# The last block's residual is added by TensorE in PSUM, and the reload's copies move behind the root

## The chip, the cores and the metric

The kernel runs on one core of a Trainium2 chip. The metric is the device time of one execution in microseconds (us), the median of several runs. In the profile PE is TensorE (PEld its weight loads), DVE is VectorE, ACT is ScalarE, POOL is GpSimd and SP is SyncE, which here issues most of the DMAs. The DMA engines are 16. "Granted clock" is the share of full clock that PE got.

## What is computed

One inference step of a two-layer streaming encoder, in float32, over 1024 prompt positions and 64 sample positions (1088 columns) of 1024 channels. Layer 0 mixes tokens by sliding-window attention, layer 1 by a diagonal state-space model; each layer then has a gated ConvFFN. Around each of the four parts stand two norms, one before, and one after it whose result is added to the residual:

```python
def rms_norm(x, g):
    x32 = x.astype(jnp.float32)
    y = x32 * lax.rsqrt(jnp.mean(x32 * x32, axis=-1, keepdims=True) + NORM_EPS) * g.astype(jnp.float32)
    return y.astype(x.dtype)
...
        hp = rms_norm(xp, g_pre_mix[i])
        ...
            mp, hrp, hip = s5_mixer(hp, h0, h0, *ssm_params)
        xp = xp + rms_norm(mp, g_post_mix[i])
        hp = rms_norm(xp, g_pre_ffn[i])
        fp, cpi = conv_ffn(hp, jnp.zeros((bp, CONV_WIDTH - 1, 2 * D_FF), hp.dtype), w_up[i], conv_w[i], conv_b[i], w_down[i])
        xp = xp + rms_norm(fp, g_post_ffn[i])
```

The change concerns two of these places: the end of layer 0 (the last line, then the first norm of layer 1, whose result the state-space mixer reads), and the end of layer 1, whose last line gives the output.

## The kernel before

Channels lie on the 128 partitions, as eight tiles `k` of 128 channels; the columns are cut into three blocks `b` of 384, 384 and 320. All weight products are float32, made of three products of a split in two parts (`mm3`, lines 224 to 226). The program is built once in Python; a scheduler then sets the order on each engine from its own estimate of times, from priorities and from `self.order(x, first)`, which puts x behind first without a wait of its own. Each engine runs its instructions in that order.

`down` ends the FFN of block 2: its last products go to PSUM tiles tagged `mm` (six buffers), and DVE adds them to `y` (L658). Then `post_norm` runs. It loads the residual in four pairs of tiles, `xs`. `rstd` squares y pair by pair on ACT (L255, L249), sums the pairs on DVE (L257, L247, L250), lets PE sum over the partitions by products with `ones` (L267, into `pr`), takes the root (L271 on ACT, where `root` is true) and refines the reciprocal on DVE (L272 to L292), and spreads it over the partitions with three transposes (L285). ACT scales y by the gain (L321). `apply` multiplies y by `pr` (L329, one pair an instruction) and adds `xs` (L332): in block 2 ahead of the mixer all four adds are DVE's, at the end the second and fourth are DVE's and the first and third POOL's; at the end each pair is then stored (L336).

Ahead of the mixer (`pre == 4` in `f`), `ssm_bounce` copies the sum into `xs[q]`, the pair's tiles with the columns in another order (L1140 on ACT for block 2), and writes them to memory `hd` (L1146); `ssm_load(q)` reloads them as `U` (L1195), 16 channels by 8 steps on the partitions. All of this is for raw values; `ssm_norm` runs a second `rstd` over the sum, spreads the root with small products (L1182, `pr<-sel`) into `rs` (L1184, L1185), and DVE multiplies `U` by it (L1203). `fill` issues products with the identity whose result nobody reads (`idle`): eight of 512 columns behind the transposes, one behind the statistics, one of 256 columns behind the small products.

The mixer then goes through 32 pairs of groups, mostly two pairs a batch: PE forms the inputs (L1258, p1), DVE scans (L1289 to L1310), PE forms the outputs (L1318, L1324), ACT copies them to `ys` (L1332). `pm` are their parameters (L1222). For each eighth of the channels `ys` is written to memory `yd` and reloaded as `yf`; ACT applies the GELU (`z`, L1359) and splits it, `zh` on ACT (L1368) and `zl` on DVE (L1372). The products of the GLU follow, then the second FFN, whose end is the end of the program.

Of the kernel before, what the change touches and what calls it, by code (L numbers as in the profile page):

```python
# [43 lines left out]
class Core:  # L44
# [193 lines left out]
    def rstd(self, src, n, tag, root, bcast=True, first=False, alt=None, adder=None, fine=False):  # L238
# [3 lines left out]
        for q in range(4):  # L242
            sq = self.n2(n, tag)
# [8 lines left out]
            if first:  # L252
                nc.gpsimd.tensor_mul(sq, xq, xq)
            else:
                self.sq[q] = nc.scalar.activation(sq, xq, AF.Square)  # L255
            if q:
                adder.tensor_add(acc, acc, sq)  # L257
            else:
                acc = sq
        else:  # L260
            adder.tensor_add(acc[:, 0], acc[:, 0], acc[:, 1])
# [8 lines left out]
        if root:  # L270
            nc.scalar.activation(x, st, AF.Sqrt, bias=self.eps)  # L271
# [40 lines left out]
    def post_norm(self, y, b, g, xsrc, root, roomy, out=None, by=None):  # L312
# [12 lines left out]
        def apply():  # L325
            last = None
            for q in range(4):
# [792 lines left out]
    def ssm_bounce(self, xt, b, qs=range(4), after=None):  # L1120
# [9 lines left out]
        for q in qs:  # L1130
            for u, v, c in segs:
                o = self.xs[q][:, :, :, c:c + (v - u) // 8]
                (pk, nk), (ps, ns), (pc, n_) = o.ap[1:]
                o = bass.AP(tensor=o.tensor, offset=self.xs[q][:, 0, 7, c:c + 1].offset, ap=[o.ap[0], [pk, nk], [pc, n_], [-ps, ns]])
                x = xt[:, 2 * q:2 * q + 2, u:v].rearrange("p k (c s) -> p k c s", s=8)
                if b < 2:
                    r = self.rn[:, 384 * b:384 * b + 384].rearrange("p (c s) -> p c s", s=8)
                    nc.vector.tensor_mul(o, x, r[:, None].to_broadcast([P, 2, 48, 8]))
                    continue
                x = nc.scalar.activation(o, x, AF.Copy)  # L1140
                if after is not None:
                    self.order(x, after[(0, 1, 3, 3)[q]])
            if b == 2:
                for k in ([0], [1]) if q == 0 else ([0, 1],):
                    r = self.hd[(2 * q + k[0]) * P:(2 * q + k[-1] + 1) * P].rearrange("(k p) s c -> p k (s c)", p=P)
                    self.hw[q] = nc.sync.dma_start(r, self.xs[q][:, k[0]:k[-1] + 1].rearrange("p k s c -> p k (s c)"))  # L1146
# [7 lines left out]
    def ssm_norm(self, xt, b):  # L1154
# [23 lines left out]
        self.fill(idle, 1, 512, self.last_st)  # L1178
        for i, c in enumerate(range(0, n, P)):
            c = min(c, n - P) // 8  # L1180
            nc.vector.tensor_scalar(ex[:, 16 * i:16 * i + 16], self.dsel, r[:, i:i + 1], None, op0=ALU.mult)
# [23 lines left out]
    def ssm(self, after):  # L1205
# [4 lines left out]
        with tc.tile_pool(name="ss", bufs=1) as sp:  # L1210
# [36 lines left out]
            def batch(qs):  # L1247
# [267 lines left out]
def build(tc, a):  # L1515
    nc = tc.nc
    with ExitStack() as ctx:
# [28 lines left out]
        def then(post, xs, xo, pre):  # L1546
# [62 lines left out]
```

## Time and profile before

| | |
|---|---|
| median of 3 runs | 2239.77 us (2237.23 to 2244.5) |
| the profiled execution, its own time | 2241.03 us |
| its span, first to last instruction | 2239.2 us |
| instructions in the span | 35982 |
| busy share PE, DVE, ACT, POOL | 98%, 74%, 47%, 18% |
| mean granted clock of PE | 0.992 |
| first FFN's last product | 1170.21 us |
| the mixer's first input products | 1190.3 us |
| last input products | 1279.9 us |
| last product of the second FFN | 2224.42 us |

Times in rows are us from the span's start. A row of a time line reads: start, length, engine, line, operation, out<-in, shape, count, and in brackets the idle time of that engine before it with what ended it. A row by stretches reads: stretch, its length, busy time of the engines asked for with the number of instructions, granted clock, DMA share, GB/s. A row of DMA issues ends with the size of one and the time to landing. On PE a float32 product counts as two instructions in the time line.

### The profile page before, as it was taken

What the parts mean: (1) busy time and instruction counts of PE and PEld (TensorE: products, weight loads), DVE (VectorE), ACT (ScalarE), POOL (GpSimd) and SP (SyncE); (2) the same over time, 40 slices, a digit from 0 to 9 for tenths busy, and PEclk for the clock granted to TensorE, in tenths of its full rate; (3) what the DMA queues carried; (4) which work ended last, traced back from release to release, by engine and by line L of the source; (5) the groups of instructions that cost most, each with busy time, mean ns of one, the idle gap of its engine ahead of it and who ended that gap; (6) DMA issues with size and microseconds to landing.
All of it is one profiled execution on the core that took longest, in us unless ns stands there. A gap on an engine that the chain in (4) does not pass through costs nothing.

```text
span 2239.2 us, 35982 instructions
## 1 busy us (share of the span) xinstructions
PE 2191.6 (98%) x13875; PEld 2117.1 (95%) x13875; DVE 1661.3 (74%) x2886; ACT 1042.3 (47%) x1890; POOL 412.8 (18%) x474
## 2 busy tenths in 40 slices
PE   9999999999999999999988899999999999999997
PEld 8987789999999999999986699999999999999997
DVE  8687647989878877767758855597976776676764
ACT  5255747422343342555545641263555455455543
POOL 5322004200032423000200034352010110110000
PEclk9999999999999999999999899999999999999999
DMA  5100015655355565887749888752266686579772
GB/s 197 37 22 29 20 62 158 241 188 202 122 150 173 176 208 187 274 279 236 233 163 339 263 280 294 249 167 75 87 224 229 218 297 226 196 272 314 218 253 97
DMA packets 208123, 428.47 MB, mean 191 GB/s; under 512 B 23312, under 2 KB 114224, under 8 KB 205008
## 3 DMA queue, kind: packets, MB, share of 16 engines
q1 hardware_dynamic: 175648, 326.56, 44.2%
q0 software_dynamic: 23984, 95.12, 11.9%
q10 hardware_dynamic: 8320, 4.49, 0.8%
q8 instruction: 109, 1.79, 0.3%
q14 instruction: 62, 0.51, 0.1%
HBM read 297.75 MB, written 128.37 MB: 190 GB/s over the span
## 4 chain that ended last, share of the span: by engine, by line
PE 32%; DMA 13%; DVE 9%; issue 4%; ACT 2%; POOL 2%; SPq 0%; DVEq 0%; ACTq 0%; POOLq 0%
PE mm L224 10%; PE mm L226 10%; PE mm L225 10%; DMA sj<-in_w_up 3%; DMA raw<-in_w_down 2%; DMA jw<-in_w_down 2%; DMA raw<-sd 1%; POOL sj L1391 1%; DMA yd<-ys 1%; DVE whl L217 1%; DMA su<-sj 1%; DMA gd<-t 1%; DVE gt L564 1%; DVE t L425 1%; DMA yf<-yd 1%
## 5 line engine op out<-in xcount | busy, mean ns | idle before, releaser
L224 PE MATMUL mm<-hl,whl 128*128 128x384 f32 (+1 forms) x1960 | 643.3, 329 | 4.1 <-DVE hl L307 3.1
L226 PE MATMUL mm<-hh,whl 128*128 128x384 f32 (+1 forms) x1960 | 641.2, 329 | 2.3 <-DVE whl L217 2.3
L225 PE MATMUL mm<-hh,whl 128*128 128x384 f32 (+1 forms) x1960 | 643.1, 328 | 0.0
L224 PEld LDWEIGHTS mm<-hl,whl 128*128 128x128 f32 x1960 | 368.4, 188 | 6.5 <-DVE hl L307 4.7
L226 PEld LDWEIGHTS mm<-hh,whl 128*128 128x128 f32 x1960 | 368.4, 188 | 3.0 <-DVE whl L217 2.9
L225 PEld LDWEIGHTS mm<-hh,whl 128*128 128x128 f32 x1960 | 368.6, 188 | 0.1
L217 DVE TENSOR_TENSOR whl<-raw,whl 128x1024 fp32r<-128x1024 f32 x202 | 254.9, 1263 | 146.7 <-ACT whl L217 146.2
L217 ACT ACTIVATE whl<-raw 128x1024 fp32r<-128x1024 f32 x202 | 213.0, 1058 | 248.1 <-PE mm L226 128.6
L224 PE MATMUL mm<-gt,whl 128*128 128x384 f32 (+1 forms) x968 | 316.8, 327 | 2.9 <-ACT whl L217 2.4
L226 PE MATMUL mm<-gt,whl 128*128 128x384 f32 (+1 forms) x968 | 315.8, 327 | 0.7 <-DVE whl L217 0.7
L225 PE MATMUL mm<-gt,whl 128*128 128x384 f32 (+1 forms) x968 | 315.9, 327 | 0.0
L224 PEld LDWEIGHTS mm<-gt,whl 128*128 128x128 f32 x968 | 181.7, 188 | 3.7 <-ACT whl L217 2.6
L226 PEld LDWEIGHTS mm<-gt,whl 128*128 128x128 f32 x968 | 181.7, 188 | 1.2 <-DVE whl L217 1.2
L225 PEld LDWEIGHTS mm<-gt,whl 128*128 128x128 f32 x968 | 181.8, 188 | 0.0
L195 DVE TENSOR_TENSOR whl<-raw,whl 128x1024 fp32r<-128x1024 f32 x84 | 96.4, 1154 | 72.7 <-ACT whl L194 71.3
L424 DVE SCALAR_TENSOR_TENSOR t<-u,ppt,t 128x1090 f32<-128x1090 f32 x88 | 126.9, 1443 | 5.8 <-ACT t L423 4.1
L194 ACT ACTIVATE whl<-raw 128x1024 fp32r<-128x1024 f32 x84 | 82.6, 987 | 101.8 <-DMA raw<-sd 40.1
L423 ACT ACTIVATE t<-u,ppt 128x1090 f32<-128x1090 f32 x88 | 114.2, 1298 | 26.2 <-DVE u L520 13.6
L425 DVE SCALAR_TENSOR_TENSOR t<-u,ppt,t 128x1090 f32<-128x1090 f32 x88 | 122.0, 1386 | 0.4
L415 DVE TENSOR_TENSOR u<-rb,mm 128x384 f32<-128x384 f32 (+1 forms) x164 | 80.8, 504 | 31.2 <-PE mm L226 26.4
L438 ACT ACTIVATE t<-t 128x1090 f32<-128x1090 f32 x44 | 49.1, 1115 | 113.1 <-DVE t L425 113.1
L564 DVE TENSOR_TENSOR gt<-gr,gt 128x768 fp32r<-128x768 f32 (+2 forms) x106 | 90.5, 881 | 11.1 <-ACT gt L563 10.2
(389 smaller groups left out, 4141.5 us busy)
## 6 DMA issues: line engine op xcount, KB each, us to landing
raw<-in_w_up SPq DMA_DIRECT2D x88, 512.0 KB, 4.4
raw<-in_w_down SPq DMA_DIRECT2D x74, 512.0 KB, 4.4
raw<-sd SPq DMA_DIRECT2D x40, 512.0 KB, 4.9
sj<-in_w_up POOLq DMA_DIRECT2D x68, 256.0 KB, 6.1
su<-sj POOLq DMA_DIRECT2D x34, 512.0 KB, 5.9
raw<-su SPq DMA_DIRECT2D x34, 512.0 KB, 4.6
pm<-prm SPq DMA_DIRECT2D x32, 522.0 KB, 8.2
gr<-td SPq DMA_DIRECT2D x40, 384.0 KB, 5.6
```

Of the source, the lines that this page charges most:

```text
L194: nc.scalar.activation(w[:, 0], raw, AF.Copy)
L195: nc.vector.tensor_sub(w[:, 1], raw, w[:, 0].bitcast(F32))
L217: x = nc.scalar.activation(w[:, 0], raw, AF.Copy), nc.vector.tensor_sub(w[:, 1], raw, w[:, 0].bitcast(F32))
L224: nc.tensor.matmul(out, w[:, 0, sl], xl, start=start, stop=False, skip_group_check=more)
L225: nc.tensor.matmul(out, w[:, 0, sl], xh, start=False, stop=False, skip_group_check=more)
L226: self.last_mm = nc.tensor.matmul(out, w[:, 1, sl], xh, start=False, stop=stop, skip_group_check=more)
L415: nc.vector.tensor_mul(u[:, t0 + 2:t0 + 2 + np_], rb[:, t0:t0 + np_], ps[:, :np_])
L423: nc.scalar.activation(t, u[:, 0:T + 2], AF.Identity, bias=cb(m), scale=cw(0, m))
L424: nc.vector.scalar_tensor_tensor(t, u[:, 1:T + 3], cw(1, m), t, op0=ALU.mult, op1=ALU.add)
L425: self.last_conv = nc.vector.scalar_tensor_tensor(t, u[:, 2:T + 4], cw(2, m), t, op0=ALU.mult, op1=ALU.add)
L438: nc.scalar.activation(ta, ta, AF.Gelu_apprx_tanh)
L564: nc.vector.tensor_sub(x[:, 1, u], raw, x[:, 0, u].bitcast(F32))
```

## The change

In block 2 ahead of the mixer and at the end (`own`) PE adds the residual for most tiles. `post_norm` takes PSUM tiles `ad` (six, at the end five); a product of the residual with the identity starts each of them, and in `apply` a product of the multiplied y with the identity is added. At the end ACT copies these tiles back to y; the rest is added by DVE, and POOL adds nothing there any more. Ahead of the mixer the second `rstd` squares the six tiles straight from PSUM, and DVE's adds of the first three pairs, which still have to reach y, stand behind the sums (first pair) and behind the small products' operands (second and third). The first tile is copied for the reload from PSUM, all others behind the root. Idle products: six of 512 columns behind the last product of y in place of eight behind the transposes, two behind the statistics in place of one. The `rd` tiles of the first batches stand behind `rs`.

```diff
-    def rstd(self, src, n, tag, root, bcast=True, first=False, alt=None, adder=None, fine=False):
+    def rstd(self, src, n, tag, root, bcast=True, first=False, alt=None, adder=None, fine=False, ads=()):
...
-            sq = self.n2(n, tag)
+            sq = self.n2(n, "sqb" if ads and q % 2 else tag)
+            if ads and q < 3:
+
+                for j in range(2):
+                    ahead = nc.scalar.activation(sq[:, j], ads[2 * q + j], AF.Square)
+                if q:
+                    adder.tensor_add(acc, acc, sq)
+                else:
+                    acc = sq
+                continue
...
+            if ads:
+                self.order(self.sq[q], ahead)
...
+        own = roomy and b == 2
+        ads = [self.mm_ps("ad")[:, :n] for _ in range(6 if out is None else 5)] if own else []
+
+        def residual(ks, first):
+            for k in ks:
+                self.order(nc.tensor.matmul(ads[k], self.ident, xs[k // 2][:, k % 2], start=True, stop=False), first)
+        if own:
+            residual(range(3), self.last_mm)
         pr, _ = self.rstd(y, n, "sqa", root, alt=b % 2 if roomy else None, fine=b == 2)
+        if own:
+            residual((3, 4), self.last_st)
+            residual(range(5, len(ads)), self.last_tr)
...
+            if own:
+                for q in range(4):
+                    yq = y[:, 2 * q:2 * q + 2]
+                    V.tensor_mul(yq, yq, pr[:, None, :n].to_broadcast([P, 2, n]))
+                    for k in range(2 * q, min(2 * q + 2, len(ads))):
+                        self.last_ad = nc.tensor.matmul(ads[k], self.ident, y[:, k], start=False, stop=True)
+                        if out is not None:
+                            nc.scalar.activation(y[:, k], ads[k], AF.Copy)
+                    if q == 3:
+                        if len(ads) < 6:
+                            V.tensor_add(y[:, 5], y[:, 5], xs[2][:, 1])
+                        V.tensor_add(yq, yq, xs[q])
+                for q in range(4 if out is not None else 0):
+                    nc.sync.dma_start(out[:, 2 * q:2 * q + 2], y[:, 2 * q:2 * q + 2])
+                return ads, xs
...
-    def ssm_bounce(self, xt, b, qs=range(4), after=None):
+    def ssm_bounce(self, xt, b, qs=range(4), ahead=None):
...
+            k0, k1 = (0, 2) if q or b < 2 else (0, 1) if ahead is not None else (1, 2)
...
-                x = nc.scalar.activation(o, x, AF.Copy)
-                if after is not None:
-                    self.order(x, after[(0, 1, 3, 3)[q]])
+                x = ahead[:, None] if ahead is not None else xt[:, 2 * q + k0:2 * q + k1]
+                x = nc.scalar.activation(o, x[:, :, u:v].rearrange("p k (c s) -> p k c s", s=8), AF.Copy)
+                if ahead is None:
+                    self.order(x, self.last_root)
...
+        ads, xs = last if b == 2 else ((), ())
+        ps, r = self.rstd(xt, n, "sqa" if b == 2 else "sqb", True, bcast=b < 2, alt=1 - b % 2, adder=nc.gpsimd if b == 0 else None, ads=ads)
         if b == 2:
-            idle = self.mm_ps("idle")
-            self.fill(idle, 8, 512, self.last_tr)
-        ps, r = self.rstd(xt, n, "sqa" if b == 2 else "sqb", True, bcast=b < 2, alt=1 - b % 2, adder=nc.gpsimd if b == 0 else None)
+            idle = self.sm_ps("idle", 0)
+            self.fill(idle, 6, 512, self.last_ad)
+            xq = xt[:, 0:2]
+            self.order(nc.vector.tensor_add(xq, xq, xs[0]), self.last_add)
...
-        self.fill(idle, 1, 512, self.last_st)
+        self.fill(idle, 2, 512, self.last_st)
...
+        for q in (1, 2):
+            xq = xt[:, 2 * q:2 * q + 2]
+            self.order(nc.vector.tensor_add(xq, xq, xs[q]), e)
...
-                    if out[0]:
-                        self.order(x, out[0])
+                    self.order(x, out[0] or self.last_rs)
...
-                c.post_norm(y, b, g(post), xs[b], post != 5 or b == 2, post in (3, 7), xo[b] if pre is None else None,
-                            {3: "1111", 7: "0101"}.get(post) if b == 2 else None)()
+                last = c.post_norm(y, b, g(post), xs[b], post != 5 or b == 2, post in (3, 7), xo[b] if pre is None else None)()
                 if pre == 4:
                     if b == 2:
-                        c.ssm_bounce(y, b, [0])
-                    c.ssm_norm(y, b)
+                        c.ssm_bounce(y, b, [0], ahead=last[0][0])
+                    c.ssm_norm(y, b, last)
                     if b == 2:
-                        c.ssm_bounce(y, b, range(1, 4), dict(c.sq))
+                        c.ssm_bounce(y, b, range(4))
```

On PE between the FFN's last product and the mixer stood (`xl` is the residual's tile, `ad` its sum's PSUM tile):

```order
L226 MATMUL mm<-gt,whl 128x320
L267 MATMUL pr<-ones,sqa 128x1 x3
L285 MATMUL pr<-ident,nvsqa 128x128 x3
L231 MATMUL idle<-ppt,ident 128x512 x8
L267 MATMUL pr<-ones,sqa 128x1 x3
L231 MATMUL idle<-ppt,ident 128x512
L1182 MATMUL pr<-sel 128x16 x3
L231 MATMUL idle<-ppt,ident 128x256
```

and stands now:

```order
L226 MATMUL mm<-gt,whl 128x320
L335 MATMUL ad<-xl,ident 128x320 x3
L278 MATMUL pr<-ones,sqa 128x1 x3
L335 MATMUL ad<-xl,ident 128x320 x2
L296 MATMUL pr<-ident,nvsqa 128x128 x3
L335 MATMUL ad<-xl,ident 128x320
L354 MATMUL ad<-y,ident 128x320 x6
L231 MATMUL idle<-ppt,ident 128x512 x6
L278 MATMUL pr<-ones,sqa 128x1 x3
L231 MATMUL idle<-ppt,ident 128x512 x2
L1224 MATMUL pr<-sel 128x16 x3
L231 MATMUL idle<-ppt,ident 128x256
```

Twelve products of 320 columns are new, and the second statistics stand behind the six idle products, which follow the last product of y.

On SP, the writes and reloads of the four pairs (`xs_10757` to `xs_10760` are pairs 0 to 3) stood, for the two first reloaded tiles:

```order
L1146 DMA hd_10756<-xs_10757 128x1096 x2
L1195 DMA U_11558<-hd_10756 128x8x137
L1146 DMA hd_10756<-xs_10758 128x2x1096
L1195 DMA U_11558<-hd_10756 128x8x137
L1146 DMA hd_10756<-xs_10759 128x2x1096
L1146 DMA hd_10756<-xs_10760 128x2x1096
L1195 DMA U_11563<-hd_10756 128x8x137 x2
L1222 DMA pm_11566<-prm_292 128x1044 x2
```

and stand now:

```order
L1185 DMA hd_10756<-xs_10757 128x1096
L1240 DMA U_11580<-hd_10756 128x8x137
L1185 DMA hd_10756<-xs_10757 128x1096
L1185 DMA hd_10756<-xs_10760 128x2x1096
L1240 DMA U_11580<-hd_10756 128x8x137
L1185 DMA hd_10756<-xs_10758 128x2x1096
L1185 DMA hd_10756<-xs_10759 128x2x1096
L1240 DMA U_11585<-hd_10756 128x8x137 x2
L1267 DMA pm_11588<-prm_292 128x1044 x2
```

Pair 3 now goes ahead of pair 1, and all but the first row wait for copies that stand behind the root.

On DVE at the end of the program stood:

```order
L291 TENSOR_TENSOR nvsqa<-nvsqa 128x3
L292 SCALAR_TENSOR_TENSOR nvsqa<-nvsqa 128x3
L329 TENSOR_TENSOR y<-y,pr 128x640 x2
L332 TENSOR_TENSOR y<-y,xl 128x640
L329 TENSOR_TENSOR y<-y,pr 128x640 x2
L332 TENSOR_TENSOR y<-y,xl 128x640
```

and stands now:

```order
L302 TENSOR_TENSOR nvsqa<-nvsqa 128x3
L303 SCALAR_TENSOR_TENSOR nvsqa<-nvsqa 128x3
L352 TENSOR_TENSOR y<-y,pr 128x640 x4
L359 TENSOR_TENSOR y<-y,xl 128x320
L360 TENSOR_TENSOR y<-y,xl 128x640
```

One add is shorter by half, and the multiplies follow each other. In the mixer's first batches PE now takes the output products of batch 4-5 ahead of half of those of batch 2-3, and the input products of batch 6-7 stand between and behind them; after these batches, and in all other parts of the program, the order is the same as before.

More of the change, by code (lines that the diff above doesn't have):

```diff
@@ L260, in rstd @@
         else:
-            adder.tensor_add(acc[:, 0], acc[:, 0], acc[:, 1])
+            self.last_add = adder.tensor_add(acc[:, 0], acc[:, 0], acc[:, 1])
         cuts = [min(c, n - P) for c in range(0, n, P)]
@@ L270, in rstd @@
         if root:
-            nc.scalar.activation(x, st, AF.Sqrt, bias=self.eps)
+            self.last_root = nc.scalar.activation(x, st, AF.Sqrt, bias=self.eps)
             nc.vector.tensor_scalar(hx, st, 1e-6, -0.5, op0=ALU.add, op1=ALU.mult)
@@ L1139, in ssm_bounce @@
                     continue
-                x = nc.scalar.activation(o, x, AF.Copy)
-                if after is not None:
-                    self.order(x, after[(0, 1, 3, 3)[q]])
+                x = ahead[:, None] if ahead is not None else xt[:, 2 * q + k0:2 * q + k1]
+                x = nc.scalar.activation(o, x[:, :, u:v].rearrange("p k (c s) -> p k c s", s=8), AF.Copy)
+                if ahead is None:
+                    self.order(x, self.last_root)
             if b == 2:
-                for k in ([0], [1]) if q == 0 else ([0, 1],):
-                    r = self.hd[(2 * q + k[0]) * P:(2 * q + k[-1] + 1) * P].rearrange("(k p) s c -> p k (s c)", p=P)
-                    self.hw[q] = nc.sync.dma_start(r, self.xs[q][:, k[0]:k[-1] + 1].rearrange("p k s c -> p k (s c)"))
+                r = self.hd[(2 * q + k0) * P:(2 * q + k1) * P].rearrange("(k p) s c -> p k (s c)", p=P)
+                self.hw[q] = nc.sync.dma_start(r, self.xs[q][:, k0:k1].rearrange("p k s c -> p k (s c)"))
     @staticmethod
```

10 lines of the change are left out of this document (5 added, 5 removed).

## The prediction

> **What bounds the kernel now.** I read the page first, then the time line of each engine at the two places that the change touches, then the DMA share and the chain behind the first place.
>
> ```profile
> span 2239.2 us, 35982 instructions
> PE 2191.6 (98%) x13875; PEld 2117.1 (95%) x13875; DVE 1661.3 (74%) x2886; ACT 1042.3 (47%) x1890; POOL 412.8 (18%) x474
> ```
>
> PE fills the span, so the change can only act where PE waits. These are the stretch from the last product of the first FFN (1170 us) through the mixer, and the 15 us at the very end. First the norm ahead of the mixer, on PE, DVE and ACT:
>
> ```profile
> 1172.21 0.80 PE L267 MATMUL pr<-ones,sqa 128*128 128x1 f32 x6 [1.70 <-DVE sqa L250]
> 1174.23 0.90 PE L285 MATMUL pr<-ident,nvsqa 128*128 128x128 f32 x3 [1.22 <-DVE nvsqa L292]
> 1174.93 8.21 PE L231 MATMUL idle<-ppt,ident 128*128 128x512 f32 x16
> 1185.34 0.83 PE L267 MATMUL pr<-ones,sqa 128*128 128x1 f32 x6 [2.20 <-DVE sqa L261]
> 1175.17 0.82 DVE L329 TENSOR_TENSOR y<-y,pr 128x640 f32<-128x640 f32 x1 [0.99 <-PE pr L285]
> 1176.77 0.81 DVE L329 TENSOR_TENSOR y<-y,pr 128x640 f32<-128x640 f32 x1
> 1184.79 0.49 DVE L261 TENSOR_TENSOR sqa<-sqa 128x320 f32<-128x320 f32 x1
> 1183.16 0.74 ACT L255 ACTIVATE sqa<-y 128x640 f32<-128x640 f32 x1 [0.89 <-DVE sqa L257]
> 1186.20 0.26 ACT L271 ACTIVATE nvsqa<-pr,eps 128x3 f32<-128x3 f32 x1
> ```
>
> The mean square of the new rows reaches PE at 1185.34, the root follows at 1186.20. Up to there the chain is four multiplies and four adds on DVE (1.60 us a pair, 1175.17 to 1176.77), with squares and sums behind them. Beside it the kernel writes those rows to memory and reloads them in another layout:
>
> ```profile
> 1178.28 0.80 SPq L1146 DMA_DIRECT2D hd<-xs  x2
> 1181.03 0.37 SPq L1195 DMA_DIRECT2D U<-hd  x1
> 1181.51 0.65 SPq L1146 DMA_DIRECT2D hd<-xs  x1
> 1182.52 0.36 SPq L1195 DMA_DIRECT2D U<-hd  x1
> 1185.20 1.50 SPq L1146 DMA_DIRECT2D hd<-xs  x2
> 1188.60 3.81 SPq L1195 DMA_DIRECT2D U<-hd  x2
> hd<-xs SPq DMA_DIRECT2D x2, 548.0 KB, 3.3
> U<-hd SPq DMA_DIRECT2D x1, 548.0 KB, 4.7
> U<-hd SPq DMA_DIRECT2D x1, 548.0 KB, 10.5
> ```
>
> The last number of the last three rows is the median time to landing: of the writes at 1178.28, of the load at 1181.03, and of the second of the loads at 1188.60 (issued at 1189.0, since a load keeps SP for 0.37 us; landed at 1199.5). It doubles because the DMA engines are full:
>
> ```profile
> 1178.90:1187.20 8.30, 6.04 (x13) 1.00 0.93 320
> 1187.20:1213.00 25.80, 21.16 (x38) 0.87 1.05 381
> 1213.00:1248.00 35.00, 26.98 (x39) 0.97 1.08 332
> 1248.00:1292.00 44.00, 42.42 (x66) 0.87 0.76 232
> 1228.95 1.03 DVE L1372 TENSOR_TENSOR zl<-z,zh 128x384 fp32r<-128x384 f32 x2 [2.52 <-ACT zh L1368]
> 1244.88 1.03 DVE L1372 TENSOR_TENSOR zl<-z,zh 128x384 fp32r<-128x384 f32 x2 [4.47 <-ACT zh L1368]
> 1219.25 14.41 DMA yd<-ys
> 1233.68 8.43 DMA yf<-yd
> ```
>
> Columns of the first four: stretch, length, DVE busy, granted PE clock, DMA share, GB/s. From 1187 to 1248 the DMA share is 1.05 and 1.08; DVE, otherwise the mixer's busiest engine, waits there twice (2.52 and 4.47 us) for a mixer output that went out and came back (the chain: 14.41 and 8.43 us). So until 1244.88 not DVE but the DMA queue sets the mixer's pace; behind it DVE does (42.42 of 44). This decides what the first half of the change is worth.
>
> **Part 1, the norm ahead of the mixer.** Six products with the identity put the residual in PSUM, six more add y. Their price is that of the idle products at full clock:
>
> ```profile
> L231 PE MATMUL idle<-ppt,ident x12: 592/592/592, 1177.8 to 1182.5; 128*128 128x512 f32 x12
> 1173.94:1177.35 3.41, 3.12 (x6) 0.51 0.75 305
> 1170.53:1173.94 3.41, 0.80 (x6) 0.99 1.01 413
> L656 ACT ACTIVATE y<-mm x16: 417/438/458, 1108.7 to 2190.9; 128x320 f32<-128x320 f32 x16
> 1196.11 1.21 PE L1324 MATMUL p<-wk,pm 64*128 64x137 f32 x16
> ```
>
> Twelve passes start 0.427 us apart (4.7 us over 11 steps); a product is two passes, 0.85 us for 512 columns and 0.54 us for 320. Three residual products (1.6 us) fit in the wait of 1.70 us ahead of the first statistics, two (1.07) in the 1.22 us ahead of the transposes, the sixth beside the first multiply: cost 0. DVE now multiplies four times without adds between (0.74 us a step). The y products follow the first multiply: from 1176.0, six times 0.54, to 1179.2. ACT copies the first tile from PSUM (0.8 us in two pieces, an estimate: twice the 0.44 us that 320 columns take from PSUM, less what overlaps), squares six tiles (six times 0.44) and then the last pair (0.74): 1176.65 to 1180.9; with two DVE sums (0.82 and 0.45) the mean square would be ready at 1182.35, three us sooner. But the order has six idle products of 512 columns between the last y product and the statistics. PE runs them in order: 1179.2 + 6 x 0.85 = 1184.4. So the statistics start at 1184.4 and not at 1182.35: 0.94 us sooner than 1185.34, the rest is held by the idle products.
>
> **Part 2, the reload behind the root.** Before, all four writes were issued from 1178.28 to 1186.3. Now only the first half of the first goes ahead (issued 1177.6, reloaded by 1184); the others' copies stand behind the root on ACT. The root ends 1.12 us behind the statistics (1185.34 to 1186.20 and 0.26 more), at 1185.5; the copy takes 0.8, and the write goes at 1186.35 and lands by 1189.1 to 1189.6 (3.3 us was the median of the two of 1178.28). In between the DMA engines idle from about 1183. Behind it all is queued without a gap, at the 381 GB/s of the row: a pair of 1096 KB in 2.88 us, 548 KB in 1.44. Pair, reload, pair, pair and two reloads are 13.0 us: the second tile's last reload lands at 1202.1 to 1202.6, against 1199.5. I take a lag of 3.0 us. By bytes it is 4.1: 8.3 us at 320 GB/s moved 2.66 MB up to 1187.2, now 1.1 MB, and 1.56 MB at 381 GB/s are 4.1. The first batches don't feel the lag (their half is reloaded by 1184), but it stays in the full queue until the output whose return frees DVE at 1244.88; behind that DVE runs without slack, and GLU's products after it. So the mixer ends 3.0 us later. Bounds: -0.94 (the return is not what sets the mixer, and the sooner statistics pass on) and +4.1.
>
> The other edits there cost nothing while that wait covers them: three residual adds on DVE (0.82 each) lie in the 1.2 us between sums and root and ahead of the reload's scale; the added idle product runs beside the root's arithmetic. One shift of order, PE taking the products of batch 4-5 ahead of half of those of batch 2-3, keeps DVE from its next batch for some 12 products (0.15 us each, from the last row above), 2 us; DVE had 7 us of waiting (2.52 + 4.47) to take that from. Without this cover the 2 us would count.
>
> **Part 3, the end.**
>
> ```profile
> 2228.45 0.81 PE L285 MATMUL pr<-ident,nvsqa 128*128 128x128 f32 x3 [1.22 <-DVE nvsqa L292]
> 2229.29 1.55 DVE L329 TENSOR_TENSOR y<-y,pr 128x640 f32<-128x640 f32 x2 [0.90 <-PE pr L285]
> 2230.88 1.58 DVE L332 TENSOR_TENSOR y<-y,xl 128x640 f32<-128x640 f32 x1
> 2233.95 1.58 DVE L332 TENSOR_TENSOR y<-y,xl 128x640 f32<-128x640 f32 x1
> 2231.80 4.18 SPq L336 DMA_DIRECT2D out_o_y<-y  x4
> out_o_y<-y SPq DMA_DIRECT2D x4, 320.0 KB, 2.3
> 2228.70:2239.20 10.50, 0.55 (x3) 0.50 0.34 125
> ```
>
> DVE's two adds take 1.58 us each, with POOL doing the other two beside them; ahead of the mixer, without POOL, a multiply and an add take 1.60 together. The last ends at 2235.53. Now DVE: four multiplies from 2229.2, 0.74 a step, one add of 320 columns (0.45) and one of 640 (0.82): 2233.4. Beside it PE adds five tiles (2230.05 + 5 x 0.54 = 2232.8) and ACT copies each out (0.44): 2233.3. The fourth output goes at about 2233.75 instead of 2235.6 and lands 2.3 us later: -1.8 us. Bounds: 0, if PE runs this at half clock (five times 1.07: 2235.4, copy 2235.9), and -2.2, if SP is not the last to be late (2233.4).
>
> Sum: 3.0 - 1.8 = +1.2 us. The profiled execution took 2241.03 us (span 2239.2), 1.26 above the median of 2239.77; I add the sum to the median: 2241.0. A difference within 0.3% (6.7 us) is about what a measurement can't tell from none.
>
> **Clock.** The row 1170.53:1173.94 has PE busy 0.80 of 3.41 us, and the next stretch runs at clock 0.51. With the five residual products in it PE is busy for some 3.3 of them, so I take full clock to 1184; how much would be enough no row shows.
> The Trainium skill, "TensorE: Matmul & The Clock Gate", section "What's actually happening", has windows of 3413 ns and half clock after an idle one. The trace agrees in the length, but its window was a quarter busy and lost the clock all the same. By the page's rule the clock stays full here and the sum is +1.2; by the stricter row it could fall, which is the last rival.
>
> **Rivals.**
> *The lag is hidden* (chance 0.22): the queue makes up the 3.0 us before 1244, by loads that were issued early. For it: of the 10.5 us to landing most is queue. Against: a DMA share over 1 for 61 us. Then only the end counts: -1.8, 2238.0.
> *The root counts* (0.16): the wait at 1244.88 is not what sets the mixer, and the first batch starts earlier: -0.94 (to -3.0 without the idle products' hold) and -1.8: 2237.0 to 2235.0. Against it are the two waits of DVE for ACT.
> *The order on PE counts as well* (0.10): if the mixer's first output goes out 2 us later and its return with it, 3.0 + 2 - 1.8 = +3.2: 2243.0.
> *Half clock* (0.10), the slow one: if five residual products don't count as busy enough, clock 0.5 from 1173.94 for two windows (6.8 us) costs PE 3.4 to 4 us of its products there: statistics at about 1188, the reload as much later, and the end gains nothing: 3.0 + 3.8 = +6.8, 2246.6. It decides from statistics at 1188.1 on (3.0 + 3.7 is the 6.7 of 0.3%).
> The forecast itself has 0.42. That the residual moves to TensorE and the statistics don't come sooner, since idle products stand ahead of them, is in it already.
>
> **Numbers.** 2241.0 for the likeliest. 2235 to 2246 takes in the bounds of both terms (-0.94 - 2.2 and +4.1 + 0) with the second and third rival, and leaves out half clock and the fast tail of the root's case. All cases but half clock lie within 0.3% of the median: 0.82 after something for their tails and for the spread of the runs (2237.23 to 2244.5); faster 0.08, from the root's case; slower 0.10, from half clock.
>
> **What would show it.** Right: statistics ahead of the mixer start right behind the sixth idle product; DMA share near 0 from about 1183 to 1187; DVE's second wait for the returned output ends near 1248 instead of 1244.88; the last output is issued 1.8 us sooner after the transposes. Wrong: statistics before 1183 or after 1186; DVE waits less than now in the mixer; granted clock 0.5 between 1174 and 1184, or at the five products of the end.

## The result and the profile after

The changed kernel takes 2251.35 us (median of 5 runs, 2248.71 to 2253.77) against 2239.77 (5 runs, 2237.23 to 2244.5): ratio 1.0054, 95% interval 1.0040 to 1.0068. It is slower by 0.54%, about 12 us. The forecast of 2241.0 was wrong, and its range (up to 2246) did not hold the time.

The page's head for the changed kernel, and the last row of the first FFN (DVE's last add of it, the row from which the offsets below are counted) in the kernel before and in the changed one:

```profile
span 2252.0 us, 36088 instructions
PE 2213.1 (98%) x13917; PEld 2134.0 (95%) x13917; DVE 1660.6 (74%) x2886; ACT 1045.4 (46%) x1900; POOL 411.6 (18%) x472
```

```profile
1170.55 0.49 DVE L658 TENSOR_TENSOR y<-y,mm 128x320 f32<-128x320 f32 x1 [2.87 <-PE mm L226]
```

```profile
1177.29 0.49 DVE L695 TENSOR_TENSOR y<-y,mm 128x320 f32<-128x320 f32 x1 [2.87 <-PE mm L226]
```

The span is 12.8 us longer, and 6.74 of that is there before the changed code begins. It is not the change. Ahead of this row every engine has the same instructions in the same order, and the profiles of the experiments, which share that part too, have the row at 1168.5 to 1175.3 (1170.25 in the run with the mixer's part of the change alone). This profile is of the slowest of the five runs (2253.77). So I count every time from that row: "+13.7" is 13.7 us behind it.

The norm ahead of the mixer, on PE, DVE, ACT and PE (time line of the changed kernel):

```profile
1185.83 5.31 PE L231 MATMUL idle<-ppt,ident 128*128 128x512 f32 x12
1190.97 0.72 PE L278 MATMUL pr<-ones,sqa 128*128 128x1 f32 x6
1188.29 0.49 DVE L272 TENSOR_TENSOR sqa<-sqa 128x320 f32<-128x320 f32 x1
1191.74 0.26 ACT L282 ACTIVATE nvsqa<-pr,eps 128x3 f32<-128x3 f32 x1 [4.65 <-PE pr L278]
```

This went as forecast. The sums are ready at 1188.78 (+11.5), PE is in the idle products until 1191, and the statistics start right behind them at +13.7, where they started at +14.8 before: 1.1 us sooner, 0.94 was forecast. ACT stands idle for 4.65 us meanwhile.

Then the writes and reloads on SP, the last reload's time to landing, and the share of the DMA engines (the last but one column) in windows of 3.41 us and, in the last row, from the landing of pair 0's second write to that of the last reload:

```profile
1184.11 0.32 SPq L1185 DMA_DIRECT2D hd<-xs  x1
1186.83 0.37 SPq L1240 DMA_DIRECT2D U<-hd  x1
1192.69 1.56 SPq L1185 DMA_DIRECT2D hd<-xs  x2
1195.77 0.37 SPq L1240 DMA_DIRECT2D U<-hd  x1
1196.50 2.34 SPq L1185 DMA_DIRECT2D hd<-xs  x2
1205.18 0.99 SPq L1240 DMA_DIRECT2D U<-hd  x2
U<-hd SPq DMA_DIRECT2D x1, 548.0 KB, 6.0
```

```profile
1184.04:1187.45 3.41, 3.41 (x12) 1.99 (x11) 3.02 (x5) 2.85 (x8) 0.00 (x0) 1.00 0.40 165
1187.45:1190.86 3.41, 3.41 (x9) 1.52 (x8) 2.03 (x3) 0.00 (x0) 0.00 (x0) 1.00 0.66 167
1190.86:1194.27 3.41, 3.41 (x19) 2.21 (x17) 2.10 (x10) 2.20 (x7) 0.99 (x7) 1.00 0.18 69
1195.71:1211.60 15.89, 11.41 (x109) 9.07 (x108) 12.84 (x23) 6.66 (x20) 0.97 (x6) 1.00 1.01 330
```

The reload of pair 1 (the last SP row, two loads) is issued at +27.9; before it was at 1188.60, +18.05. Its second load is issued at 1205.59 and takes the 6.0 us of the row below that: it lands at 1211.6 (+34.3) instead of 1199.5 (+29.0). In the first three windows, 10 us, the DMA engines were at 0.4 on the average, and near 0, as forecast, from 1190.3 to 1193.2 (0.01). The granted clock in these windows is 1.00, as forecast.

What I did not forecast comes 20 us further on. DVE's waits over 1.5 us between 1202 and 1264, and PE in the place of the longest:

```profile
1202.41 0.50 DVE L1248 TENSOR_TENSOR U<-U,sel 128x328 f32<-128x328 f32 x1 [2.18 <-DMA U<-hd]
1223.65 0.72 DVE L1333 TENSOR_TENSOR wk<-pm,p 128x548 f32<-128x548 f32 x1 [8.88 <-PE p L231]
1231.71 0.73 DVE L1333 TENSOR_TENSOR wk<-pm,p 128x548 f32<-128x548 f32 x1 [2.73 <-PE p L231]
1246.03 1.03 DVE L1416 TENSOR_TENSOR zl<-z,zh 128x384 fp32r<-128x384 f32 x2 [1.76 <-ACT zh L1412]
1262.26 1.03 DVE L1416 TENSOR_TENSOR zl<-z,zh 128x384 fp32r<-128x384 f32 x2 [4.77 <-ACT zh L1412]
```

```profile
1214.14 0.79 PE L1368 MATMUL p<-wk,pm 64*128 64x137 f32 x2 [1.91 <-DVE wk L1353]
1214.87 1.18 PE L1303 MATMUL p<-U,pm 128*64 128x137 f32 x8
1215.98 0.82 PE L1362 MATMUL p<-U,pm 128*128 128x137 f32 x2
1216.73 1.74 PE L1368 MATMUL p<-wk,pm 64*128 64x137 f32 x6
1218.40 0.83 PE L1362 MATMUL p<-U,pm 128*128 128x137 f32 x2
1219.16 2.19 PE L1368 MATMUL p<-wk,pm 64*128 64x137 f32 x8
1221.28 1.18 PE L1303 MATMUL p<-U,pm 128*64 128x137 f32 x8
1222.39 1.16 PE L231 MATMUL p<-ppt,ident 128*128 128x238 f32 x2
```

The last row of DVE is its second wait for a returned output; it ends at +85.0, where the forecast had about +77 (+74.3 before). The first is a wait for the second half of pair 0, which landed at +25.1 instead of +19.7. The longest, 8.88 us, is new: DVE needs the input products of batch 6-7 (L1303 with the idle product behind). In PE's queue they now stand, in two halves, behind and between products of batch 4-5's scan result (L1368), and PE can't begin those before DVE has made that result (1.91 us of waiting for DVE L1353). So DVE, then PE, then DVE run one after the other, where PE used to be a batch ahead. The same place in the two programs (`p1` are input products, `p3` output products, `wk` scan results; `p1_11707` before and `p1_11729` now are of batch 6-7, `wk_11656` and `wk_11678` of batch 2-3, `wk_11722` of batch 4-5), before:

```
L1258 MATMUL p1_11707<-U_11558,pm_11566 64x137 x8
L231 MATMUL p1_11707<-ppt_91,ident_83 128x238
L1318 MATMUL p3_11779<-U_11558,pm_11555 128x137
L1318 MATMUL p3_11780<-U_11558,pm_11555 128x137
L1324 MATMUL p3_11722<-wk_11656,pm_11552 128x137
```

and now:

```
L1368 MATMUL p3_11745<-wk_11678,pm_11574 128x137 x4
L1368 MATMUL p3_11802<-wk_11722,pm_11577 128x137
L1303 MATMUL p1_11729<-U_11580,pm_11588 64x137 x4
L1362 MATMUL p3_11857<-U_11580,pm_11588 128x137
L1368 MATMUL p3_11802<-wk_11722,pm_11577 128x137 x3
L1362 MATMUL p3_11802<-U_11580,pm_11577 128x137
L1368 MATMUL p3_11802<-wk_11722,pm_11577 128x137 x4
L1303 MATMUL p1_11729<-U_11580,pm_11588 64x137 x4
L231 MATMUL p1_11729<-ppt_91,ident_83 128x238
```

And these products ran at half clock. Windows of the changed kernel (length, PE busy and its count first; the granted clock is the third number from the right):

```profile
1208.52:1211.94 3.42, 2.78 (x18) 2.34 (x18) 3.35 (x7) 0.49 (x2) 0.19 (x1) 1.00 1.11 352
1211.94:1215.35 3.41, 1.50 (x8) 0.99 (x9) 2.76 (x3) 2.29 (x7) 0.00 (x0) 0.50 1.03 408
1215.35:1218.76 3.41, 3.41 (x17) 2.54 (x14) 0.00 (x0) 0.76 (x2) 0.00 (x0) 0.50 1.02 392
1229.00:1232.42 3.42, 3.42 (x19) 2.47 (x18) 0.71 (x2) 0.00 (x0) 0.00 (x0) 0.50 0.84 219
1232.42:1235.83 3.41, 3.41 (x34) 2.82 (x32) 3.24 (x5) 1.05 (x5) 0.25 (x2) 1.00 0.93 267
```

GLU's first product, before and now:

```profile
1294.44 0.44 PE L224 MATMUL pb<-zl,whl 128*128 128x384 f32 x1 [0.55 <-ACT ys L1332]
```

```profile
1310.87 0.44 PE L224 MATMUL pb<-zl,whl 128*128 128x384 f32 x1 [0.54 <-ACT ys L1376]
```

It stands at +123.9 before and +133.6 now: in this profile the mixer cost 9.7 us. Not all of that stays: the span ends at +1074.7 against +1068.7, some 6 us late, after the end of the program (below) gave back 1.0. The end of the program, on PE and SP, with the outputs' median time to landing:

```profile
2242.24 0.54 PE L296 MATMUL pr<-ident,nvsqa 128*128 128x128 f32 x3
2245.60 2.52 SPq L362 DMA_DIRECT2D out_o_y<-y  x4
out_o_y<-y SPq DMA_DIRECT2D x4, 320.0 KB, 2.5
```

From the transposes to SP's last issue it is 5.88 us (2242.24 to 2248.12) against 7.53 (2228.45 to 2235.98): 1.65 sooner, 1.8 was forecast. But the span ends 9.76 us behind the transposes against 10.75, which is only 1.0 sooner: the four outputs now leave within 2.5 us and not 4.2, and the last takes 2.98 us to land instead of 2.33.

### The profile page after: what moved, and what is told of

Same layout as the page of the kernel before. It is cut to its first block, busy times and chain, and to the rows that moved or that the text cites. A ratio compares the mean times of both kernels' runs of the same rounds, so it can differ in the third digit from the quotient of the medians.

```text
span 2252.0 us, 36088 instructions
## 1 busy us (share of the span) xinstructions
PE 2213.1 (98%) x13917; PEld 2134.0 (95%) x13917; DVE 1660.6 (74%) x2886; ACT 1045.4 (46%) x1900; POOL 411.6 (18%) x472
## 4 chain that ended last, share of the span: by engine, by line
PE 46%; DMA 7%; DVE 5%; ACT 2%; issue 1%; POOL 0%; SPq 0%; ACTq 0%; DVEq 0%; POOLq 0%
PE mm L224 12%; PE mm L226 12%; PE mm L225 12%; DMA raw<-in_w_down 2%; PE pb L224 1%; PE pb L226 1%; PE pa L225 1%; PE pb L225 1%; PE pa L226 1%; PE pa L224 1%; DMA yd<-ys 1%; PE p L1368 1%; DMA yf<-yd 1%; DMA gr<-gd 1%; DMA raw<-sd 1%
## 5 line engine op out<-in xcount | busy, mean ns | idle before, releaser
L195 DVE TENSOR_TENSOR whl<-raw,whl 128x1024 fp32r<-128x1024 f32 x84 | 96.4, 1154 | 75.7 <-ACT whl L194 75.2
```

Of the source, the lines that this page charges most:

```text
L195: nc.vector.tensor_sub(w[:, 1], raw, w[:, 0].bitcast(F32))
```

## The experiments

Two theories. **Order:** the mixer loses because PE takes batch 6-7's input products too late (and at half clock). **Lag:** it loses because the copies behind the root make the reloads late, and the full DMA queue keeps that lateness. The expectations call pairs 0 to 3 the first to fourth tile. The ratios compare with the kernel before; 0.1% is 2.2 us.

| run | ratio to before | 95% interval |
|---|---|---|
| the change | 1.0054 | 1.0040 to 1.0068 |
| end alone | 1.0003 | 0.9993 to 1.0012 |
| mixer alone | 1.0055 | 1.0042 to 1.0069 |
| change, PE's order as before | 1.0029 | 1.0015 to 1.0043 |
| kernel before, late copies alone | 1.0028 | 1.0016 to 1.0039 |
| change, early copies | 1.0006 | 0.9994 to 1.0019 |

**The two halves of the change.** First the end alone: the kernel before with the new `post_norm`, and there

```
-        own = roomy and b == 2
+        own = roomy and b == 2 and out is not None
```

> The kernel before with the change at the end of the program alone (five tiles added by TensorE, copied out by ACT). Both theories of the mixer say nothing here. In the changed kernel the stretch from the last transpose to the end of the span is 9.76 us against 10.75, so the end is worth -1.0: 2238.8 us. Two readings of the 6.7 us that the changed kernel is late already at 1170 us are told apart: if they lie in the addresses and the length of any changed program they appear here too (2245); if they vary from one execution to the next, or come with the mixer's edits, this profile is at the old time at 1170.

Ratio 1.0003. Its profile has the row that ends the FFN at 1173.22, so the 6.7 us are spread between executions, within what these profiles show. Its last output is issued and landed as in the changed kernel (SP's row there is 2235.76 2.52). The 1.0 us is in the profile but too small for the times. A warning also came from it: its mixer is that of the kernel before, and yet GLU began at +127.4 and not +123.9. Single profiles of the same mixer differ by 3.5 us there, so below the ratios decide, and offsets only tell where. Between lies a wait of 4.19 us for the split of GLU's first weight, which the profile of the kernel before did not have:

```profile
1284.91 1.22 DVE L217 TENSOR_TENSOR whl<-raw,whl 128x1024 fp32r<-128x1024 f32 x1 [4.19 <-ACT whl L217]
```

Then the mixer alone, with `out is None` in that place:

> The changed kernel with the end as before. The mixer's part of the change by itself: the changed profile is 9.75 us late at GLU's first product against the start of the mixer, and gives 2.7 of it back by 1805 us. Both theories of the mixer (order on PE, lag of the reload): 2239.8 + 7 = 2247, or with the 6.7 us that lie ahead of the mixer 2252 to 2253. If it comes out at 2240, the loss is not in the mixer's edits.

Ratio 1.0055, the whole loss. DVE's wait is there again, 8.87 us and then 2.72 (and a third of 3.55).

**PE's order.** The changed kernel, with `p1x` the list of each batch's last input product and `me` the batch's number in it (from 1):

```
+                                if c == 0 and s == 0 and me + 1 < len(p1x):
+                                    self.order(x, p1x[me + 1])
```

> The changed kernel, with PE's queue in the mixer put back: the products of a batch's scan results stand behind the first products of the batch two further on, as before; the copies for the reload stay behind the root. Order theory: DVE's wait of 8.88 us for the first products of batch 6-7 goes (to under 2 us), so does the one of 2.73 after it, PE is not held at half clock from 1212 to 1232, and the time falls by some 9 us to 2242 (3 us of lag may remain). Lag theory: the late reload and the full DMA queue set the pace, the wait only changes its name (to the loads of pm or U): 2249 to 2252. The 6.7 us ahead of the mixer, if they belong to the program, stay in either case.

Ratio 1.0029: about half of the loss went, and half stayed. DVE's rows in this run, and its first product of GLU:

```profile
1210.09 0.73 DVE L1335 TENSOR_TENSOR wk<-pm,p 128x548 f32<-128x548 f32 x1 [2.03 <-PE p L231]
1234.70 1.03 DVE L1420 TENSOR_TENSOR zl<-z,zh 128x384 fp32r<-128x384 f32 x2 [5.17 <-ACT zh L1416]
1248.21 1.03 DVE L1420 TENSOR_TENSOR zl<-z,zh 128x384 fp32r<-128x384 f32 x2 [2.05 <-ACT zh L1416]
1287.08 1.23 DVE L217 TENSOR_TENSOR whl<-raw,whl 128x1024 fp32r<-128x1024 f32 x1 [4.59 <-ACT whl L217]
1302.43 0.44 PE L224 MATMUL pb<-zl,whl 128*128 128x384 f32 x1 [0.54 <-ACT ys L1380]
1213.00:1226.00 13.00, 13.00 (x153) 10.60 (x152) 11.09 (x16) 7.01 (x24) 0.70 (x5) 1.00 1.12 291
```

The wait of 8.88 is 2.03, the 2.73 is gone, and the clock is whole from 1213 on (last row; from 1199 to 1213 its mean was 0.76). So the order is a cause, and what it costs is 0.25% (1.0054 less 1.0029), with an uncertainty of 0.2 from both intervals: some 5.6 us, less than the 9.6 us by which the two waits fell. Part of the waiting moved: DVE waits 5.17 us for the first returned output (2.52 before). The wait for the second ends at 1248.21, +77.8 against +74.3: 3.5 us late. Then DVE waits 4.59 us for the split of GLU's first weight, and GLU begins at +132.0. The run of the end alone, with the old mixer, has 4.19 us of the same wait and GLU at +127.4, so an early reload can show this wait too, and nothing here ties it to the late one.

**The copies.** The changed kernel, with the copies taken tile by tile (six of the eight from PSUM) behind the last square:

```
-                if ahead is None:
-                    self.order(x, self.last_root)
+                for k in range(k0, k1):
+                    y = ads[2 * q + k] if 2 * q + k < 6 else xt[:, 2 * q + k]
...
+                    if ahead is None:
+                        self.order(x, self.sq[3])
```

> The changed kernel, with the copies for the reload taken from PSUM tile by tile, behind the last square instead of behind the root, in the 4 us in which ACT waits for the statistics. The writes go 4 to 5 us sooner, and PE's queue in the mixer comes out nearly as before by itself. Lag theory and order theory both: the mixer is no later than before, DVE does not wait for batch 6-7, 2251 - 10 = 2241 (with 6.7 us ahead of the mixer), or 2236 without them. With the run on the order it tells the two apart: order theory has both at about the same time (within 3 us), lag theory has only this one fast. If the copies delay the squares, the statistics come later than 1190.97 less the 6.7 us, and some of it is lost.

Ratio 1.0006: the loss is gone. SP issues pair 1's reload at +18.6, DVE's second return and GLU's first product are at +75.2 and +125.1:

```profile
1187.35 4.01 SPq L1241 DMA_DIRECT2D U<-hd  x2
1243.89 1.03 DVE L1417 TENSOR_TENSOR zl<-z,zh 128x384 fp32r<-128x384 f32 x2 [4.74 <-ACT zh L1413]
1293.79 0.44 PE L224 MATMUL pb<-zl,whl 128*128 128x384 f32 x1 [0.54 <-ACT ys L1377]
```

PE's order came out nearly as before here without being told to, so the other order had come with the late copies. The lag alone (the run on the order) leaves about half of the loss, and this run removes both; no run has the order alone, with an early reload. The statistics are as early as in the changed kernel (+13.7); what that 1.1 us is worth is too small for these times to show.

**The late copies alone.** The kernel before, with

```
-                    self.order(x, after[(0, 1, 3, 3)[q]])
+                    self.order(x, self.last_root)
```

and the order of PE held as above:

> The kernel before, with one thing of the change alone: the copies of the second to fourth tile (and with them writes and reloads) stand behind the root; the first tile goes ahead as before, nothing is added by TensorE, and PE takes the products of a batch's scan behind the first products of the batch two on, as it did. Lag theory: the second tile's last reload lands 3 to 6 us later than 29.0 us behind the FFN's last row, and the time is 2244 to 2248. If the loss needs the other edits of the norm (products of the residual, moved idle products): 2240.

Ratio 1.0028. With no sum in PSUM and no idle product moved, the lag is worth 6.3 us (3.6 to 8.7 by the interval). Pair 0 goes ahead whole here. Pair 1's reload landed at +32.3, 3.4 us late:

```profile
1195.03 2.97 SPq L1195 DMA_DIRECT2D U<-hd  x2
1302.43 0.45 PE L224 MATMUL pb<-zl,whl 128*128 128x384 f32 x1 [0.54 <-ACT ys L1336]
```

GLU's first product stands at +128.5: 4.6 us later than in the profile of the kernel before, but only 1.1 later than in that of the end alone. Where the 6.3 us arise can't be read from one profile. Lag (0.28 here, 0.29 in the run on the order) and order (0.25) make up the change's 0.54%.

**How the lag is carried on.** First, is it pair 3's write that goes ahead of pair 1's? The run on the order, with pair 3's copies ordered behind pair 2's:

```
+                    if q == 3:
+                        self.order(x, self.last_copy)
+                    self.last_copy = x
```

> The kernel of the run on the order (PE's queue as before, copies behind the root), with one more order: the fourth tile's copy and write go behind those of the second and third. In the changed kernel SP writes the fourth tile (1096 KB) ahead of the second, since its residual is added first. Lag theory: the second tile's last reload lands some 3 us sooner against the last row of the FFN (34.6 us in the run on the order, 29.0 before), and the time falls by 2 to 3 us, from 2248 to 2245. If the amount of data in the queue counts and not which write is first: 2248.

Missed. The reload was issued only 1.1 us sooner (+27.0) and landed later, at +36.1, beside pair 3's write, which was then still in the queue (landed at +32.5). Ratio 1.0020 (1.0009 to 1.0032), not told apart from 1.0029. So it is not pair 3's place ahead of pair 1 that makes the reload late.

Second, the queue itself: the run on the order without `self.spill()`. It leaves out the write of the last block's rows, and the next norm reads others in their place (`xd[0]`), as many bytes:

> The kernel of the run on the order (PE's queue as before, copies behind the root: 0.29% over the kernel before), without the write of the last block's rows to memory in the mixer (1.31 MB at 381 GB/s: 3.4 us of the full DMA queue; the next norm reads as many bytes from the rows of the norm before; that write is left out). Queue theory (the late reload costs time because it stays in a full queue): both returned outputs come 3 us sooner than in the run on the order, GLU starts as much sooner, and the ratio to before falls from 1.0029 to 1.0013 to 1.0018. If the lag does not go through the queue (it is a round trip or DVE's own order), the ratio stays at 1.003, as the copies-first kernel did not change without that write.

Ratio 1.0015 (1.0002 to 1.0028): in the middle of what the queue theory said, but its interval overlaps that of 1.0029. Second return and GLU are at +74.7 and +127.6, 3.1 and 4.5 us sooner than in the run on the order:

```profile
1232.24 1.03 DVE L1419 TENSOR_TENSOR zl<-z,zh 128x384 fp32r<-128x384 f32 x2 [5.90 <-ACT zh L1415]
1243.62 1.02 DVE L1419 TENSOR_TENSOR zl<-z,zh 128x384 fp32r<-128x384 f32 x2
1296.46 0.44 PE L224 MATMUL pb<-zl,whl 128*128 128x384 f32 x1 [0.54 <-ACT ys L1379]
```

Third, GLU's first two weights, whose loads stand on SP behind the fifth returned output. Three batches sooner (`qs[-1] == 25` for `qs[-1] == 31` in `batch`), in the run on the order and in the run without the write:

> The kernel of the run on the order (PE's queue as before, copies behind the root: 2248), with GLU's first two weight loads three batches sooner. There the second return was 3.5 us late and GLU 8.1, with 4.59 us of waiting for a weight between. Weights theory: GLU is late by 3.5 to 4 only, 2248 - 4 = 2244. If the returns set GLU's start: 2248.

> The same, with GLU's first two weight loads issued three batches sooner. Queue and weights theory together: the lag at the second return is under 1 us and no wait for a weight is left, the ratio to before is 1.000 to 1.001. If the weights' wait is only where other slack shows: as the run without the write.

Ratios 1.0018 (1.0006 to 1.0029) and 1.0008 (0.9994 to 1.0022). In the first the wait of 4.59 is 1.46, and GLU begins 3.3 us sooner (+128.7). In the second the wait (2.95 without the write) is gone, but GLU begins no sooner (+127.4 against +127.6): DVE waits 2.91 us for a returned output instead. The ratios of both steps go the way of the theory, but each step alone is within its interval; both together (1.0029 to 1.0008) are 4.7 us of 6.5, with an uncertainty of about as much (0.2%).

**Can it be made faster?** With the early copies, the copies of pairs 0 and 1 ahead of the squares:

> The kernel of the run with the early copies, with the copies of the first two tiles ahead of the squares on ACT (the other two behind the last square). The second tile's last reload lands 28 us behind the last row of the FFN (30.3 in the run with the early copies, 29.0 before). Lag theory: the first waits of DVE get shorter by 1 to 2 us and the time is 2238, 2 below the kernel before; half a us of it is the end. If the reload is no longer what counts once it is as early as before: 2239 to 2240, as with the early copies. The squares come later by the copies (some 2 us), and the six idle products cover that: statistics stay at 13.7 us behind the last row.

Ratio 0.9991 (0.9978 to 1.0004). From this kernel, three more: without the write, with three idle products instead of six, and with the weights sooner; and the last two together.

> The kernel of the run with the copies first, without the write of the last block's rows to memory in the mixer (1.31 MB; the next norm reads the rows of the norm before in their place, as many bytes). It leaves that write out. Queue theory (the full DMA queue sets the mixer's pace up to the second returned output): 1.31 MB at 381 GB/s are 3.4 us, both returned outputs come 3 us sooner, DVE's waits for them shrink from 2 and 4.7 us, GLU starts 3 us sooner and the time is 2235 to 2236. If DVE or the round trip of the output sets it: 2238 to 2240, as the run with the copies first.

> The kernel of the run with the copies first, with three idle products of 512 columns behind the last y product in place of six (and PE's queue in the mixer held as it is). PE comes free 2.6 us sooner, the statistics then start when the sums are ready, 1 to 2 us sooner. Queue theory: the root is not what the mixer waits for, the time is that of the run with the copies first (within 1 us). If the root counts: 1 to 2 us less. If the idle products were needed for the clock: granted clock 0.5 in one or two windows ahead of the first products of the mixer, and 1 to 3 us more.

> The kernel of the run with the copies first, with GLU's first two weight loads issued three batches sooner, so that SP takes them ahead of the fifth returned output. In the run with the copies first DVE's wait for the second return ended 3.1 us sooner than before, and GLU began 1.7 us later, with a wait of 4.26 us on DVE for the split of the first weight, whose load stood on SP behind the fifth return. Weights theory: that wait goes, GLU starts 3 to 4 us sooner, 2235 to 2236. If the weights' wait is only the place where DVE's slack shows (the returned outputs set GLU's start): 2239, and the wait appears for a returned output or a product.

> The run with three idle products (2238.4), with GLU's first two weight loads three batches sooner. Its profile had no wait of DVE for a weight over 2 us, so the weights theory gives little here: 2237 to 2238.5. If the two edits add up as in the other runs 2235.

Ratios 0.9990 (0.9977 to 1.0003), 0.9991 (0.9979 to 1.0003), 0.9998 (0.9985 to 1.0011) and 0.9999 (0.9987 to 1.0012). None beats the kernel before by more than the measurement can tell. Without the write, the second return came at +68.2 instead of +71.2 and GLU at +122.5 instead of +125.5, the 3 us expected, and the ratio did not follow. So leaving out the write brings the returns 3 us sooner whether the reload is late or early. Three idle products brought the statistics only 0.6 us sooner. The weights sooner took the wait for a weight away (4.26 us; GLU at +121.1 instead of +125.5), and the time did not follow either: for the kernel with early copies both theories failed, or the gain was lost in the spread. Two of these ratios can differ by 0.18%, 4 us, by chance.

## Why the prediction was wrong

- **Statistics and clock ahead of the mixer:** right. The idle products held the statistics to 1.1 us sooner (forecast 0.94), what the root gained can't be seen in the times, the clock stayed whole from 1174 to 1184 (here 1181 to 1191).
- **"I take a lag of 3.0 us":** mis-sized. Pair 1's reload landed 5.3 us late (5.7 in the run on the order), above the bound of 4.1. The step "Behind it all is queued without a gap, at the 381 GB/s of the row" failed, and in its second half. From the landing of pair 0's second write (1195.71) to the last reload (1211.60) 15.9 us passed in the changed kernel, not 13.0 (16.0 in the run on the order). The queue had no gap in them (DMA share 1.01, the last row of windows on the norm above), but it moved 330 GB/s: what takes 13.0 us at 381 GB/s takes 15.0 at 330 (an estimate from the two rates). Why the rate was lower here no run shows. "The first batches don't feel the lag" failed too: DVE waited 2.18 us for the second half of pair 0.
- **"It stays in the full queue until the output … behind that DVE runs without slack":** the first half fits the run on the order (3.5 us late at the second return), and leaving out 1.31 MB moved that return by 3.1 us, as a full queue would. The second half is not borne out as a size: the lag cost 6.3 us in the time instead of 3.0, and the two runs that measure it have 3.0 just outside their intervals (from 3.4 and 3.6 us on). The run on the writes' order, with a reload as late, has 4.5 us and an interval that holds 3.0. More transfers stand behind the second return (six more returned outputs, and GLU's weights behind the fifth), and DVE waited 4.59 us for the first weight, but 4.19 in an execution of the old mixer as well. So how 3.5 us at the return become 6.3 in the time, or whether they do beyond the spread, stays open.
- **"One shift of order … 2 us; DVE had 7 us of waiting … to take that from":** the term that was furthest off, some 5.6 us (1 to 10 by the intervals) instead of 0. I counted 12 products at 0.15 us that were moved ahead, and not what they wait for. They need DVE's own result of batch 4-5, so the shift took away PE's lead of a batch and DVE waited 8.88 us. The clock fell to half as well. That the order counts was among the rivals, but with 2 us and a chance of 0.10.
- **End:** -1.0 instead of -1.8; the issue was as forecast, the landing not. In the times it can't be seen.
- Taken with measured sizes, the same sum is 6.3 + 5.6 - 1.0 = +10.9, against 12 measured (9 to 15). The 5.6 is itself a difference from the changed kernel, so the sum checks little more than that the 6.3 agrees with the 6.5 us left in the run on the order.

What stays open: how much of the 5.6 us is the half clock and how much the wait. The products from 1214.87 to 1223.48 would take 4.3 us at full clock instead of 8.6 (an estimate, half of it), so the wait would be some 4.5. No run separates the two. Nor is it settled whether a rest of the lag remains (1.0008, an interval that holds 1).

## What to carry to other kernels

When a step is moved, look in the order of every engine that waits for it at the first instruction that now stands ahead of another, and ask what that one itself waits for: a shift of 12 products cost some 5.6 us because their operand came from the engine that was waiting. A lateness that enters a full queue need not be paid once at the next known wait: here 3.4 us at the reload cost 6.3 us (3.6 to 8.7). Before a wait in one profile is called new, look for it in a second execution of the old program. And a statistic that is ready 1.1 us sooner does not repay what was moved behind it (here the copies) if the stage waits for that.

## What the runs showed of the hardware that I had not expected

The clock. In the rows above, a window with PE busy for 2.78 of 3.42 us is followed by half clock, while the prediction's window with 0.80 of 3.41 is too, and PE then stays at 0.50 for six windows, five of them with PE busy throughout, until 1232.42. The Trainium skill, "TensorE: Matmul & The Clock Gate", section "What's actually happening", has the full clock back after one busy window of about 3.4 us. The trace does not agree, if a window in which the profile shows PE busy throughout is a busy one: five such windows were not enough here. At half clock PE shows as busy throughout with half as many products (17 against 34 in the rows), so its busy share does not tell which windows count. And one window may not decide alone: the three ahead of the one of 2.78 had PE busy for 2.30, 2.09 and 2.00 us, at full clock. What decides no run here shows.

The same instructions end the first FFN at 1168.5 to 1177.3 us in the profiles of this study, a spread of 8.8 us (0.4%), larger than most differences sought here. And one profile (the run on the writes' order) records a mean clock of 0.941 over the span and is no longer for it (2244.5 us).
